# Paired score banks, B's values with 256 moving queries, and A's row sums applied after the values product

## The chip, the cores and the metric

The kernel runs on one core of a Trainium2 chip. The metric is the device time of one execution in microseconds (us), the median of several runs. All times here are us unless marked ns.

## What is computed

Two layers of an encoder over a sequence of S = 512 tokens with D = 1024 channels. Each layer has an attention part with two groups of heads and a gated feed-forward part (ConvGLU). What matters here is the attention part, shortened:

```python
h = rmsnorm(x, g_attn)
# h @ w_in gives q, k, v of group A and of group B; q, k get a per-head norm and rotary
# group A: 8 query heads, 2 key heads, dim 64, each block of 128 queries sees keys of 1 block to either side
scores = where(valid, q @ k.T * 64**-0.5, NEG)
m = maximum(max(scores), sink)
p = exp(scores - m)
p = p / (sum(p) + exp(sink - m))
out_a = p @ v
# group B: 4 heads, two score maps each (dim 64), values of dim 128, all 512 keys
p = softmax(q @ k.T * 64**-0.5)          # two maps: p0, p1
out_b = (p0 - lam * p1) @ v              # then a per-head norm, times a gain
x = x + concat(out_a, out_b) @ w_out
x = x + down(silu(conv(up_gate(norm(x)))) * up_value(norm(x)))
```

## The kernel before

**Arithmetic.** Every product is fp32 kept as a high and a low part (float32r), three matmuls for one (`mm3`, L193: high by high, high by low, low by high). `split_out` (L245) makes the two parts of a tile: ACT copies the source into the high part, DVE subtracts to get the low part. Where the source lies in PSUM, its bank is free only when both have read it. The residual is held transposed, eight tiles of 128 channels by 512 tokens. Weights come by DMA in units; ACT rounds a unit to its high part (L181) and DVE or POOL makes the low part (L182).

**Who sets the order.** Each engine runs its instructions in one fixed order. A scheduler sets it from the order in which the code emits them and from when their inputs and buffers come free in its own model of time. `weave` (L121) decides the order of emission: attention (`attend`, L580, with the weight `ATT` = 92) is mixed with a second track of weight 98.6, which is projection work for group B's two halves (`proj_b`, L614: values bv, queries bq, keys bk, four blocks of 128 tokens each) and then the output projection (`out_pass`, L627, passes 0 and 1; `out_tail`, L660). Each track yields numbers for the PE time of its pieces, and the one that is behind goes next. So matmuls of the second track (names pj_bv, pj_bq, pj_bk, wo) stand between attention's matmuls and fill the time in which attention waits.

**Group A** (L399 to L477) goes over two pairs of heads `ip` and four query blocks `qb`. `a_scores` writes four score tiles sc_a, each in a PSUM bank of its own (`at`), from 64-row matmuls: heads g = 0 and 1 lie in rows 0 to 63 and 64 to 127. DVE adds the mask and takes the maximum (L416), ACT takes the exponentials with their sums (so_a, L434), DVE adds the sink's exponential es_a and inverts the sums, and four DVE multiplications normalise the probabilities (L441). `a_values` transposes them on PE (pt_a, L457), splits them, multiplies by the values into pv_a, and splits pv_a by halves of 64 rows into yh and yl.

**Group B** (L488 to L577) goes over halves of two heads, query blocks and heads. `b_scores` writes two score tiles sc_b (L502), DVE takes two maxima (L505), ACT two exponentials (e_b, L509), DVE combines them (L517). `b_values` transposes the result (wt_b, L529), splits it and multiplies it with the values, the transposed probabilities stationary and 128 columns of values moving (L538 to L541). `b_norm` sums the squares on DVE, multiplies by the inverse root, transposes (tr_yb, L566) and splits.

**PSUM.** Eight banks of 128 x 512: `mm` two (projection and output projection), `at` four single ones (scores, A's and B's transposes), `acc` one (sums of a values product), `tq` one (transposes). The projection's queries and keys pass through `qk_out` (L324): ACT copies the product into raw (L331), which frees the mm bank, and squares it (L333); DVE sums; POOL takes the power -0.5 (L243); DVE multiplies keys by it (L342); POOL does the rotary (L348, L352, L353); PE transposes into the tq bank (tr_bq, tr_bk, L357), and `split_out` reads that bank.

**SBUF buffers** of interest: rp 7 tiles of 128 x 256, tmp 7 of 128 x 512, prob 6, yp 3.

## Time and profile before

| | |
|---|---|
| runs | 1309.32, 1310.32, 1308.12, median 1309.32 |
| profiled execution, its span from first to last instruction | 1302.4 |
| instructions in it | 17571 |
| PE busy in the span | 98% |
| DVE, ACT, POOL busy in the span | 59%, 43%, 30% |
| mean DMA rate | 79 GB/s |

The profile shows one execution. Its span is all of that execution's time that is shown; the median of the runs is 6.9 longer than it. A row of a timeline is: start, duration, engine, line of the kernel, operation, output <- inputs, shape. A row of a group adds the count and, after the bar, busy time and mean ns of one, and then idle time of the engine ahead of it and what ended it. xN marks records that lie on each other and were put into one. PE is TensorE (its matmuls are pipelined, and their ends are modelled, so starts are the better guide), PEld its weight loads, DVE the vector engine, ACT the scalar engine, POOL the GpSimd engine, SP the queue that issues DMAs.

### The profile page before, as it was taken

What the parts mean: (1) busy time and instruction counts of PE and PEld (TensorE: products, weight loads), DVE (VectorE), ACT (ScalarE), POOL (GpSimd) and SP (SyncE); (2) the same over time, 40 slices, a digit from 0 to 9 for tenths busy, and PEclk for the clock granted to TensorE, in tenths of its full rate; (3) what the DMA queues carried; (4) which work ended last, traced back from release to release, by engine and by line L of the source; (5) the groups of instructions that cost most, each with busy time, mean ns of one, the idle gap of its engine ahead of it and who ended that gap; (6) DMA issues with size and microseconds to landing.
All of it is one profiled execution on the core that took longest, in us unless ns stands there. A gap on an engine that the chain in (4) does not pass through costs nothing. (4 is left out here: it accounts for less than half of the span.)

```text
span 1302.4 us, 17571 instructions
## 1 busy us (share of the span) xinstructions
PE 1270.6 (98%) x6744; PEld 1056.6 (81%) x6744; DVE 772.9 (59%) x1425; ACT 557.5 (43%) x1027; POOL 385.4 (30%) x446
## 2 busy tenths in 40 slices
PE   6999899999999999999999999999899999999998
PEld 6988788687888888888899878877788888888887
DVE  7678787767655324554466786767765543355532
ACT  4566555435433223333455656544443332233321
POOL 6847376114211000110156654741411110011100
PEclk8999999999999999999999999999999999999999
DMA  5211112113332233332331211111133322433232
GB/s 181 91 33 49 58 33 65 33 33 97 98 97 85 85 106 97 98 97 79 100 98 66 65 33 33 56 59 33 33 113 97 97 81 94 117 98 98 79 106 90
DMA packets 32628, 102.96 MB, mean 79 GB/s; under 512 B 3616, under 2 KB 4000, under 8 KB 32544
## 3 DMA queue, kind: packets, MB, share of 16 engines
q1 hardware_dynamic: 32544, 101.84, 25.6%
q8 instruction: 53, 0.87, 0.3%
q14 instruction: 31, 0.25, 0.1%
HBM read 99.73 MB, written 2.10 MB: 78 GB/s over the span
## 5 line engine op out<-in xcount | busy, mean ns | idle before, releaser
L181 ACT CAST wh<-wr 128x1024 fp32r<-128x1024 f32 (+3 forms) x210 | 197.7, 944 | 400.1 <-PE up L195 192.0
L195 PE MATMUL up<-nf_l,wh 128*128 128x512 f32 x704 | 275.3, 391 | 2.3 <-DVE nf_l L213 1.9
L196 PE MATMUL up<-nf_h,wl 128*128 128x512 f32 x704 | 274.5, 390 | 1.2 <-DVE wl L182 0.9
L194 PE MATMUL up<-nf_h,wh 128*128 128x512 f32 x704 | 272.9, 390 | 0.0
L182 DVE TENSOR_TENSOR wl<-wr,wh 128x1024 fp32r<-128x1024 f32 (+3 forms) x174 | 193.3, 1114 | 112.2 <-ACT wh L181 111.8
L702 POOL TENSOR_TENSOR cv<-cv,rb 128x512 f32<-128x512 f32 x44 | 57.8, 1316 | 521.5 <-ACT cv L701 521.5
L195 PEld LDWEIGHTS up<-nf_l,wh 128*128 128x128 f32 x704 | 132.1, 188 | 33.6 <-DVE nf_l L213 6.6
L196 PEld LDWEIGHTS up<-nf_h,wl 128*128 128x128 f32 x704 | 132.1, 188 | 29.7 <-DVE wl L182 2.9
L194 PEld LDWEIGHTS up<-nf_h,wh 128*128 128x128 f32 x704 | 132.2, 188 | 27.6
L195 PE MATMUL dn<-act,wh 128*128 128x512 f32 x352 | 138.5, 394 | 0.0
L196 PE MATMUL dn<-act,wl 128*128 128x512 f32 x352 | 138.4, 394 | 0.0
L194 PE MATMUL dn<-act,wh 128*128 128x512 f32 x352 | 137.9, 393 | 0.0
L182 POOL TENSOR_TENSOR wl<-wr,wh 128x1024 fp32r<-128x1024 f32 x36 | 87.1, 2421 | 89.4 <-ACT wh L181 89.4
L695 DVE TENSOR_TENSOR gp<-up,rb 128x512 f32<-128x512 f32 x44 | 30.3, 693 | 103.4 <-PE up L196 101.8
L703 DVE TENSOR_TENSOR cv<-cv,up 128x512 f32<-128x512 f32 x44 | 30.2, 687 | 82.6 <-POOL cv L702 73.0
L194 PEld LDWEIGHTS dn<-act,wh 128*128 128x128 f32 x352 | 66.0, 188 | 16.0
L195 PEld LDWEIGHTS dn<-act,wh 128*128 128x128 f32 x352 | 66.0, 187 | 15.7
L196 PEld LDWEIGHTS dn<-act,wl 128*128 128x128 f32 x352 | 66.0, 188 | 15.4
L716 DVE TENSOR_TENSOR x<-x,dn 128x512 f32<-128x512 f32 x32 | 22.0, 689 | 78.4 <-PE dn L196 78.4
L509 ACT ACTIVATE e_b<-sc_b,mx_b,rqb 128x512 f32<-128x512 f32 x64 | 49.2, 774 | 38.6 <-DVE mx_b L506 38.6
L701 ACT ACTIVATE cv<-cv 128x512 f32<-128x512 f32 x44 | 27.8, 632 | 76.4 <-DVE cv L700 76.3
L505 DVE TENSOR_REDUCE mx_b<-sc_b 128x1 f32<-128x512 f32 x64 | 42.0, 681 | 0.2
(211 smaller groups left out, 2713.7 us busy)
## 6 DMA issues: line engine op xcount, KB each, us to landing
wr<-w_up SPq DMA_DIRECT2D x88, 512.0 KB, 3.6
wr<-w_in SPq DMA_DIRECT2D x36, 512.0 KB, 3.7
wr<-w_down SPq DMA_DIRECT2D x32, 384.0 KB, 3.1
wr<-w_down SPq DMA_DIRECT2D x32, 320.0 KB, 2.9
wr<-w_out SPq DMA_DIRECT2D x16, 512.0 KB, 3.6
x<-xT SPq DMA_DIRECT2D x8, 256.0 KB, 5.3
outT<-x SPq DMA_DIRECT2D x8, 256.0 KB, 2.0
rows<-row_par SPq DMA_DIRECT2D x2, 260.0 KB, 5.0
```

Source lines behind the costliest of these rows:

```text
L181: nc.scalar.copy(hi[:, o], raw[:, o])
L182: eng.tensor_tensor(out=lo[:, o], in0=raw[:, o], in1=hi[:, o], op=ALU.subtract)
L194: nc.tensor.matmul(acc, lhsT=a[0], rhs=b[0], start=start, stop=False)
L195: nc.tensor.matmul(acc, lhsT=a[0], rhs=b[1], start=False, stop=False)
L196: nc.tensor.matmul(acc, lhsT=a[1], rhs=b[0], start=False, stop=stop)
L505: nc.vector.tensor_reduce(out=mx[:, c:c + 1], in_=sc[c], axis=AX, op=ALU.max)
L509: nc.scalar.activation(e[c], sc[c], AF.Exp, bias=mx[:, c:c + 1], scale=rq[:, c:c + 1], accum_out=lsum[:, 2 * j + c:2 * j + c + 1])
L695: nc.vector.tensor_tensor(out=g[:, 1:S + 1], in0=acc[0], in1=rb, op=ALU.mult)
L701: nc.scalar.activation(cv, cv, AF.Silu)
L702: nc.gpsimd.tensor_tensor(out=cv, in0=cv, in1=rb, op=ALU.mult)
L703: nc.vector.tensor_tensor(out=cv, in0=cv, in1=acc[1], op=ALU.mult)
L716: nc.vector.tensor_tensor(out=x_sb[d], in0=x_sb[d], in1=acc, op=ALU.add)
```

## The change

- The four single `at` banks become two pairs (`at2`, a tile over two banks). The two 64-row score tiles of a step, in A and in B, lie in one pair, and one DVE reduction takes B's two maxima. The feed-forward part and the projections that used `at` take halves of a pair.
- Group A: the normalisation of the probabilities is gone. POOL copies the four inverse sums over 64 columns each (rx_a); after the values product PE turns rx_a by two plain fp32 matmuls with the identity (rt_a, in tq, L481 of the changed kernel), ACT copies that to SBUF (ry_a), DVE multiplies it with pv_a by halves (L487), and one split over 128 rows makes yh and yl. A's transposes pt_a go to a half of a pair for the first key block, to tq for the second, to mm for the third.
- Group B: the order of steps is now half, pair of query blocks, head, block in the pair. `b_weights` transposes and splits; `b_values` then multiplies once for two query blocks, values stationary and 256 moving columns. `b_norm` handles two query blocks and both heads at once: ACT scales and squares, PE sums the squares by four matmuls with a column of ones (ss_yb, L578), POOL takes the power, PE spreads the factors over rows by four matmuls (rt_yb, L586), DVE multiplies, and the split reads SBUF. The transposes tr_yb are gone.
- The output projection's gates wait on pairs of query blocks; tmp has 8 buffers, prob 4 of double size, the rotary tables share 3, yp is gone.

```diff
-        return sb.tile([P, S], F32R, tag="prob", bufs=6, name=name)
+        return sb.tile([P, 2, S], F32R, tag="prob", bufs=4, name=name)
...
-        return sb.tile([P, n], F32, tag="tmp", bufs=7, name=name)
+        return sb.tile([P, n], F32, tag="tmp", bufs=8, name=name)
...
-    def at(name):
-        return ps.tile([P, S], F32, tag="at", bufs=4, name=name)
+    def at2(name):
+        return ps.tile([P, 2, S], F32, tag="at", bufs=2, name=name)
...
+    def both(name):
+        t = at2(name)
+        return t[:, 0], t[:, 1]
...
-                sc = [at(f"sc_{nm}_{i}_{g}") for g in range(2)]
+                sc = both(f"sc_{nm}_{i}")
...
-            for i in range(4):
-                nc.vector.tensor_scalar(out=so[i][:, :n], in0=so[i][:, :n], scalar1=rl[:, i:i + 1], scalar2=None,
-                                        op0=ALU.mult)
-            a_so[ip, qb] = so
+            rx = rp(f"rx_{nm}")
+            nc.gpsimd.tensor_copy(rx.rearrange("p (i d) -> p i d", d=HD), rl.unsqueeze(2).broadcast_to([P, 4, HD]))
+            a_so[ip, qb] = so, rx
         def a_values(ip, qb):
             kb0, kb1 = max(qb - 1, 0), min(qb + 2, NT)
...
-            so = a_so.pop((ip, qb))
+            so, rx = a_so.pop((ip, qb))
...
-                tr = at(f"pt_{nm}_{b}")
+                tr = mm(f"pt_{nm}_{b}") if b == 2 else both(f"pt_{nm}_{b}")[0] if b == 0 else tq(f"pt_{nm}_{b}")
...
-                ph = prob(f"ph_{nm}_{b}")
-                pl = prob(f"pl_{nm}_{b}")
-                split_out(ph, pl, tr)
-                pb.append((ph, pl))
+                pt = prob(f"p_{nm}_{b}")
+                split_out(pt[:, 0], pt[:, 1], tr)
+                pb.append((pt[:, 0], pt[:, 1]))
...
+            rt = tq(f"rt_{nm}")
+            for i in range(2):
+                nc.tensor.matmul(rt[:, i * P:(i + 1) * P], lhsT=rx[:, i * P:(i + 1) * P], rhs=ident,
+                                 start=True, stop=True)
+            ry = tmp(f"ry_{nm}")
+            nc.scalar.copy(ry[:, :CW], rt[:, :CW])
             for g in range(2):
                 rs = slice(g * HD, (g + 1) * HD)
-                o = slice(qb * P, (qb + 1) * P)
-                split_out(ya[ip][0][rs, :, o], ya[ip][1][rs, :, o],
-                          pv[rs, g * 2 * P:(g + 1) * 2 * P].rearrange("p (a q) -> p a q", q=P))
+                nc.vector.tensor_tensor(out=ry[rs, CW:], in0=ry[rs, :CW], in1=pv[rs, g * CW:(g + 1) * CW], op=ALU.mult)
+            o = slice(qb * P, (qb + 1) * P)
+            split_out(ya[ip][0][:, :, o], ya[ip][1][:, :, o], ry[:, CW:].rearrange("p (a q) -> p a q", q=P))
+            yield 0.25
...
-            if j == 0:
-                b_st[half, qb] = small(f"bl{l}_{half}_{qb}", 4)
...
-            sc = [at(f"sc_{nm}_{c}") for c in range(2)]
+            sc2 = at2(f"sc_{nm}")
+            sc = (sc2[:, 0], sc2[:, 1])
             for i, (u, v) in enumerate(((0, 0), (0, 1), (1, 0))):
                 for c in range(2):
                     rs = slice(c * HD, (c + 1) * HD)
                     nc.tensor.matmul(sc[c], lhsT=q[u][rs, j, qb * P:(qb + 1) * P], rhs=k[v][rs, j, :],
                                      start=i == 0, stop=i == 2)
-            for c in range(2):
-                nc.vector.tensor_reduce(out=mx[:, c:c + 1], in_=sc[c], axis=AX, op=ALU.max)
+            nc.vector.tensor_reduce(out=mx, in_=sc2, axis=AX, op=ALU.max)
...
-        def b_values(half, qb, j):
+        def b_weights(half, qb, j):
             h = 2 * half + j
...
             w = b_st.pop((half, qb, j))
-            tr = (mm if half and j else at)(f"wt_{nm}")
+            if qb % 2 == 0:
+                b_st[half, j, "w"] = [prob(f"w{n}_b{l}_{h}_{qb}").rearrange("p a (b q) -> p (a b) q", b=2)
+                                      for n in "hl"]
+            wt = b_st[half, j, "w"]
+            tr = (mm(f"wt_b{l}_{h}_{qb}") if half and j else both(f"wt_b{l}_{h}_{qb}")[0])
             for b in range(NT):
                 nc.tensor.transpose(tr[:, b * P:(b + 1) * P], w[:, b * P:(b + 1) * P], ident)
-            wh, wl = prob(f"wth_{nm}"), prob(f"wtl_{nm}")
-            split_out(wh, wl, tr)
+            o = slice(qb % 2 * P, qb % 2 * P + P)
+            split_out(wt[0][:, :, o], wt[1][:, :, o], tr.rearrange("p (b q) -> p b q", b=NT))
             yield 0.5
...
+
+        def b_values(half, qp, j):
+            if j == 0:
+                b_st[half, qp, "acc"] = accum(f"yb{l}_{half}_{qp}")
+            yb = b_st[half, qp, "acc"][:, j * CW:(j + 1) * CW]
+            wt = b_st.pop((half, j, "w"))
+            for b in range(NT):
+                vh, vl = (v[:, b % 2 * CW + j * P:b % 2 * CW + j * P + P] for v in vb[half, b // 2])
+                mm3(yb, (vh, vl), (wt[0][:, b], wt[1][:, b]), b == 0, b == NT - 1)
+                if b % 2:
+                    yield 0.7
+
+        def b_norm(half, qp):
+            nm = f"yb{l}_{half}_{qp}"
+            yb = b_st.pop((half, qp, "acc"))
+            y = tmp(f"y_{nm}")
+            nc.scalar.activation(y, yb, AF.Copy, scale=cols[:, l, c3:c3 + 1])
+            sq = tmp(f"sq_{nm}")
+            nc.scalar.activation(sq, yb, AF.Square)
+            le = small(f"le_{nm}", 4)
+            lsum = b_st.pop((half, qp)).rearrange("p (i c) -> p i c", c=2)[:, :, 0]
             nc.vector.scalar_tensor_tensor(out=le, in0=lsum, scalar=EPS / (1.0 - lam_init) ** 2, in1=lsum,
                                            op0=ALU.mult, op1=ALU.mult)
...
+            yield 0.2
+            ss = tq(f"ss_{nm}")
+            for i in range(4):
+                nc.tensor.matmul(ss[:, i:i + 1], lhsT=sq[:, i * P:(i + 1) * P], rhs=ones, start=True, stop=True)
+            rr = small(f"rr_{nm}", 4)
+            nc.vector.scalar_tensor_tensor(out=rr, in0=ss[:, :4], scalar=1.0 / (P * (1.0 - lam_init) ** 2), in1=le,
+                                           op0=ALU.mult, op1=ALU.add)
+            rsqrt(rr, rr)
+            yield 0.5
+            rt = tq(f"rt_{nm}")
+            for i in range(4):
+                nc.tensor.matmul(rt[:, i * P:(i + 1) * P], lhsT=rr[:, i:i + 1].broadcast_to([P, P]), rhs=ident,
+                                 start=True, stop=True)
+            nc.vector.tensor_tensor(out=y, in0=y, in1=rt, op=ALU.mult)
+            if qp == 0:
...
+            yh, yl = (v[:, :, qp * CW:(qp + 1) * CW] for v in b_st[half, "y"])
+            split_out(yh, yl, y.rearrange("p (j q) -> p j q", j=2))
+            b_st["yb", half, qp] = True
+            yield 0.5
         def attend():
             seq = [("a", qb, ip) for ip in range(2) for qb in range(NT)]
-            seq += [(half, qb, j) for half in range(2) for qb in range(NT) for j in range(2)]
+            seq += [(half, 2 * qp + i, j) for half in range(2) for qp in range(2) for j in range(2) for i in range(2)]
...
-                    yield from b_values(kind, qb, j)
-                    while norms:
-                        yield from norms.pop(0)
-                    if j == 1:
-                        norms.append(b_norm(kind, qb))
-                        yield next(norms[0])
+                    return
+                yield from b_weights(kind, qb, j)
+                if norms:
+                    yield from norms.pop(0)
+                if qb % 2:
+                    yield from b_values(kind, qb // 2, j)
+                    if j:
+                        g = b_norm(kind, qb // 2)
+                        yield next(g)
+                        norms.append(g)
...
-            yield lambda: ("ya" if p == 0 else ("yb", 0, NT - 1)) in b_st
+            yield lambda: ("ya" if p == 0 else ("yb", 0, 1)) in b_st
...
-            yield lambda: ("yb", 1, 2 * half + 1) in b_st
+            yield lambda: ("yb", 1, half) in b_st
...
-            yield lambda: ("yb", 1, 1) in b_st
+            yield lambda: ("yb", 1, 0) in b_st
```

What this does to the order. PE's order in the first layer, where group A's steps (sc_a, pv_a, pt_a, rt_a) stand among group B's projection (pj_bk, and the transposes tr_bq of its queries). Before:

```order
L412 MATMUL sc_a_1_1_0_1_1508<-ka_213,qal_1_418 128x384
L195 MATMUL pj_bk_1_1519<-wl_1101,na_h_139 128x256
L357 MATMUL tr_bq_2_1320<-ident,raw_bq_2_1308 128x128 x2
L196 MATMUL pj_bk_1_1519<-wh_1100,na_l_140 128x256
L194 MATMUL pj_bk_1_1519<-wh_1100,na_h_143 128x256
L194 MATMUL pv_a_0_3_1421<-ph_a_0_3_0_1427,va_214 128x512
L195 MATMUL pj_bk_1_1519<-wl_1101,na_h_143 128x256
L196 MATMUL pj_bk_1_1519<-wh_1100,na_l_144 128x256
L194 MATMUL pj_bk_1_1519<-wh_1100,na_h_147 128x256
L195 MATMUL pj_bk_1_1519<-wl_1101,na_h_147 128x256
```

And after, at the transposes of the same block of queries:

```order
L208 MATMUL pj_bk_1_1483<-wh_1084,na_l_148 128x256
L369 MATMUL tr_bq_2_1302<-ident,raw_bq_2_1290 128x128 x2
L481 MATMUL rt_a_0_2_1326<-ident,rx_a_0_2_1056 128x128 x2
L369 MATMUL tr_bq_3_1371<-ident,raw_bq_3_1359 128x128 x2
L469 MATMUL pt_a_0_3_0_1430<-ident,so_a_0_3_0_0_1176 128x128
L469 MATMUL pt_a_0_3_0_1430<-ident,so_a_0_3_1_0_1187 128x128
L469 MATMUL pt_a_0_3_0_1430<-ident,so_a_0_3_0_1_1178 128x128
L469 MATMUL pt_a_0_3_0_1430<-ident,so_a_0_3_1_1_1189 128x128
L469 MATMUL pt_a_0_3_1_1438<-ident,so_a_0_3_0_0_1176 128x128
```

Before, projection matmuls stand on both sides of tr_bq_2; after, tr_bq_2, A's rt_a, tr_bq_3 and pt_a follow each other, and tr_bq_2, rt_a, tr_bq_3 and the second pt_a share the one tq bank.

ACT's order at the copy raw_bk_0, which frees the mm bank of the first block of B's keys, with A's exponentials (so_a) and copies. Before:

```order
L246 CAST yh_0_779<-pv_a_0_2_1252 64x2x128
L331 ACTIVATE raw_bk_0_1480<-pj_bk_0_1443,na_r 128x256
L333 ACTIVATE sq_bk_0_1482<-raw_bk_0_1480 128x256
L246 CAST ph_a_0_3_0_1427<-pt_a_0_3_0_1422 128x512
L431 ACTIVATE es_a_1_0_1407<-dn_a_1_0_1405 128x4
L434 ACTIVATE so_a_1_0_0_0_1357,ls_a_1_0_1409<-so_a_1_0_0_0_1357,ng_a_1_0_1402,rqa_413 128x256
L434 ACTIVATE so_a_1_0_0_1_1359,ls_a_1_0_1409<-so_a_1_0_0_1_1359,ng_a_1_0_1402,rqa_413 128x256
```

After:

```order
L258 CAST bqh_0_792<-tr_bq_2_1302 128x2x128
L484 COPY ry_a_0_2_1329<-rt_a_0_2_1326 128x256
L258 CAST bqh_0_792<-tr_bq_3_1371 128x2x128
L258 CAST yh_0_775<-ry_a_0_2_1329 128x2x128
L258 CAST p_a_0_3_0_1435<-pt_a_0_3_0_1430 128x512
L258 CAST p_a_0_3_1_1443<-pt_a_0_3_1_1438 128x512
L444 ACTIVATE es_a_1_0_1417<-dn_a_1_0_1415 128x4
L447 ACTIVATE so_a_1_0_0_0_1343,ls_a_1_0_1419<-so_a_1_0_0_0_1343,ng_a_1_0_1412,rqa_411 128x256
L447 ACTIVATE so_a_1_0_0_1_1345,ls_a_1_0_1419<-so_a_1_0_0_1_1345,ng_a_1_0_1412,rqa_411 128x256
L447 ACTIVATE so_a_1_0_1_0_1383,ls_a_1_0_1419<-so_a_1_0_1_0_1383,ng_a_1_0_1412,rqa_411 128x256
L447 ACTIVATE so_a_1_0_1_1_1385,ls_a_1_0_1419<-so_a_1_0_1_1_1385,ng_a_1_0_1412,rqa_411 128x256
L343 ACTIVATE raw_bk_0_1458<-pj_bk_0_1399,na_r 128x256
```

The copy raw_bk_0 stood ahead of A's exponentials and now stands behind them and behind six copies.

PE's order at the start of group B's second half (scores sc_b_2 and sc_b_3, weights' transposes wt_b, output projection wo). Before:

```order
L529 MATMUL wt_b_0_3_2809<-ident,e_b_0_3_0_2588 128x128 x4
L502 MATMUL sc_b_3_0_0_2856<-bkh_1_1785,bqh_1_1783 128x512
L566 MATMUL tr_yb_0_1_2694<-ident,y_yb_0_1_2565 128x128 x2
L502 MATMUL sc_b_2_0_0_2782<-bkl_1_1786,bqh_1_1783 128x512
L502 MATMUL sc_b_2_0_1_2783<-bkl_1_1786,bqh_1_1783 128x512
L502 MATMUL sc_b_2_0_0_2782<-bkh_1_1785,bql_1_1784 128x512
L502 MATMUL sc_b_2_0_1_2783<-bkh_1_1785,bql_1_1784 128x512
L502 MATMUL sc_b_3_0_0_2856<-bkl_1_1786,bqh_1_1783 128x512
L502 MATMUL sc_b_3_0_0_2856<-bkh_1_1785,bql_1_1784 128x512
L194 MATMUL wo_0_5_2988<-yh_0_779,wh_2379 128x512
```

After:

```order
L522 MATMUL sc_b_3_0_2779<-bkh_1_1747,bqh_1_1745 128x512 x2
L522 MATMUL sc_b_3_0_2779<-bkl_1_1748,bqh_1_1745 128x512 x2
L522 MATMUL sc_b_3_0_2779<-bkh_1_1747,bql_1_1746 128x512 x2
L548 MATMUL wt_b_2_0_2807<-ident,e_b_2_0_0_2682 128x128 x4
L578 MATMUL ss_yb_0_1_2820<-ones,sq_yb_0_1_2774 128x1 x4
L522 MATMUL sc_b_3_1_2837<-bkh_1_1747,bqh_1_1745 128x512 x2
L522 MATMUL sc_b_3_1_2837<-bkl_1_1748,bqh_1_1745 128x512 x2
L522 MATMUL sc_b_3_1_2837<-bkh_1_1747,bql_1_1746 128x512 x2
L548 MATMUL wt_b_2_1_2869<-ident,e_b_2_1_0_2718 128x128 x4
L548 MATMUL wt_b_3_0_2931<-ident,e_b_3_0_0_2788 128x128 x4
L206 MATMUL wo_0_6_2945<-yh_0_775,wh_2640 128x512
L207 MATMUL wo_0_6_2945<-yl_0_776,wh_2640 128x512
```

Before, the scores' matmuls of two heads were mixed, with output-projection matmuls (wo_0_5) behind the first of them; after, the two row halves of one score follow each other as one row with x2, and the output projection (wo_0_6) stands behind all four scores.

More of the change, by code (lines that the diff above doesn't have):

```diff
@@ L34 @@
 RP = 7
-YP = 3
 SMP = 12
@@ L376, in akv_done @@
             qk_out(raw[:, :P], t, P, tabs[1], ka, "ka", None)
-        run(project("akv", akv_done, at))
+        run(project("akv", akv_done, halves(both)))
         rqa = sb.tile([P, NT, 4, 2], F32, tag="rqa", bufs=1, name=f"rqa{l}")
@@ L387 @@
         qk = {}
-        banks = iter((mm, mm, at, at, at, at, mm, mm))
+        pairs_at = halves(both)
+        banks = iter((mm, mm, pairs_at, pairs_at, pairs_at, pairs_at, mm, mm))
         run(proj_a(0, lambda name: next(banks)(name)))
@@ L666 @@
               (chain(proj_b(0), proj_b(1), out_pass(0, mm), out_pass(1, mm), out_tail()), 98.6))
-        run(out_last(1, w_last, wide))
+        run(out_last(1, w_last, halves(wide2)))
         norm.square(NK - 2)
@@ L707 @@
             last = pi == len(FF_PARTS) - 1
+            wide = halves(wide2)
             for d in range(NK):
```

79 lines of the change are left out of this document (22 added, 57 removed).

## The prediction

> **What bounds the kernel now.** I read the page's busy shares first, then the table by stretches of 100 us, then the timeline inside the attention stretches, then the tile views of what passes through the few PSUM banks there. The shares:
>
> ```profile
> PE 1270.6 (98%) x6744; PEld 1056.6 (81%) x6744; DVE 772.9 (59%) x1425; ACT 557.5 (43%) x1027; POOL 385.4 (30%) x446
> ```
>
> PE is busy 98% of the span, so the end is set by what PE has to issue plus the time in which it waits. The stretches that the change touches, columns PE, PEld, DVE, ACT, POOL, granted clock, DMA share, GB/s:
>
> ```profile
> 100.00:200.00 100.00, 95.80 (x652) 80.19 (x652) 79.76 (x194) 58.70 (x147) 64.18 (x67) 1.00 0.15 46
> 200.00:300.00 100.00, 95.81 (x532) 75.52 (x532) 73.44 (x150) 49.22 (x100) 34.46 (x28) 0.98 0.16 48
> 700.00:800.00 100.00, 97.78 (x663) 83.36 (x662) 73.83 (x216) 60.32 (x154) 49.72 (x47) 0.98 0.17 51
> 800.00:900.00 100.00, 98.25 (x585) 78.90 (x583) 70.90 (x163) 53.01 (x118) 50.18 (x45) 0.98 0.14 43
> 900.00:1000.00 100.00, 96.50 (x490) 79.92 (x489) 68.30 (x102) 44.46 (x68) 24.97 (x31) 0.98 0.25 75
> ```
>
> Even here PE is busy: its idle time is 4.20 + 4.19 + 2.22 + 1.75 + 3.50 = 15.9 us. So work taken from DVE, ACT or POOL gains nothing by itself, work taken from PE counts in full, and a new wait of PE costs in full unless other work stands in PE's order at that place. DVE is at 70 to 80% in these stretches, so a chain through DVE, ACT and POOL is long, and only PE's filler hides it.
>
> **What PE loses and gains.** Ends of matmuls are modelled, so I price by the distance between starts. The values product before, moving 128, and a product with 256:
>
> ```profile
> 240.85 0.28 PE L539 MATMUL yb<-vb,wth_b 128*128 128x128 f32 x1
> ...
> 241.52 0.28 PE L539 MATMUL yb<-vb,wth_b 128*128 128x128 f32 x1
> ...
> 281.25 0.40 PE L649 MATMUL wo<-yl_b,wh 128*128 128x256 f32 x2
> 281.49 0.40 PE L649 MATMUL wo<-yh_b,wh 128*128 128x256 f32 x2
> ```
>
> Six steps take 0.67, so 0.111 each; two of 256 take 0.24, so 0.120 each. B's values go from 384 matmuls of 128 to 192 of 256: 42.6 to 23.0, **-19.6**.
>
> Score matmuls, first alone between wide products, then of both row halves together:
>
> ```profile
> 243.02 0.40 PE L194 MATMUL wo<-yh,wh 128*128 128x512 f32 x1
> 243.34 0.49 PE L502 MATMUL sc_b<-bkh,bqh 64*128 64x512 f32 x1
> 243.68 0.39 PE L502 MATMUL sc_b<-bkl,bqh 64*128 64x512 f32 x1
> 243.91 0.39 PE L502 MATMUL sc_b<-bkh,bql 64*128 64x512 f32 x1
> 244.24 0.50 PE L195 MATMUL wo<-yl,wh 128*128 128x512 f32 x1
> ...
> 154.82 0.72 PE L502 MATMUL sc_b<-bkh,bqh 64*128 64x512 f32 x2
> 155.16 0.62 PE L502 MATMUL sc_b<-bkl,bqh 64*128 64x512 f32 x2
> 155.39 0.61 PE L502 MATMUL sc_b<-bkh,bql 64*128 64x512 f32 x2
> ```
>
> A slot is 0.23 (243.68 to 243.91), and two matmuls of different row halves share one (155.16 to 155.39 with x2). Going from 128 rows to 64 and back lengthens three steps, to 0.32, 0.34 and 0.33, so by 0.09 + 0.11 + 0.10 = about 0.29 an episode. In the order, before has 58 such pairs and 268 single ones in 114 episodes, after has 190 pairs and 4 single ones in 58. B's slots go from 167 to 97: 70 x 0.23 = -16.2. A's go from 159 to 97; at 256 or 384 moving columns I take 0.148, between 0.120 and 0.175 (midway between 0.12 and 0.23): 62 x 0.148 = -9.2. Episodes: 56 x 0.29 = -16.1. Together **-41.5**.
>
> Added: 32 matmuls that turn A's reciprocals (L481), 32 that sum B's squares (L578) and 32 that spread B's factors (L586), in plain fp32. The nearest row:
>
> ```profile
> 317.79 1.05 PE L673 MATMUL rps<-ident,nf_r 128*128 128x128 f32 x8
> ```
>
> Four matmuls of the code are eight passes there; the record covers seven steps and a last duration of 0.27, so (1.05 - 0.27) / 7 = 0.111 a pass. 96 matmuls are 192 passes, +21.3; B's 32 transposes go, -3.6. Sum **+17.7**; were the sums of squares, which move one column, to cost nothing, it would be 10.6, and I keep the upper end because the short matmuls above pay 0.111 whether they move 128 or twice that. PE's issue changes by -19.6 - 41.5 + 17.7 = **-43.4**, with ends at -50.5 and, were the halves not to run together, -43.4 + 25.4 = -18.
>
> **What comes off DVE.** The four normalisations of A's probabilities (L441) and some small sums go:
>
> ```profile
> L441 DVE TENSOR_SCALAR so_a<-so_a,rl_a 128x256 f32<-128x256 f32 (+1 forms) x64 | 36.9, 636 | 0.0
> ```
>
> 36.9 us off a DVE that isn't the bound: nothing by itself. It shortens the step from A's reciprocals to its transposes, which is counted in the chains below.
>
> **The waits that come in.** Before, four single banks, two mm banks and one tq bank serve attention and projections. After, the four are two pairs; A's transposes of the second key block, A's reciprocal matmuls and the q/k transposes of the projection all pass through the one tq bank; and in the order after they stand next to each other on PE with no projection matmul between (the rows in the section on the change). Each must wait until the one before it has been read twice:
>
> ```profile
> L246 ACT CAST bqh<-tr_bq x16: 352/372/374, 95.8 to 827.3; 128x256 fp32r<-128x256 f32 x16
> L247 DVE TENSOR_TENSOR bql<-tr_bq,bqh x16: 406/414/425, 96.8 to 827.7; 128x256 fp32r<-128x256 f32 x16
> ```
>
> Transposes 0.11 + 0.27, copy 0.37, subtraction 0.41, with the hand-overs 1.25 us at the least. The second chain is on ACT: raw_bk_0, which frees the mm bank that the next projection needs, now stands behind six copies, the sink's exponential and four exponentials of A. What the chain is made of:
>
> ```profile
> L416 DVE CUSTOM_DVE_ANT_0 so_a<-sc_a,mask_sb 128x256 f32<-128x256 f32 x15 | 6.0, 409 | 0.4 <-PE pt_a L457 0.4
> L247 DVE TENSOR_TENSOR pl_a<-pt_a,ph_a 128x512 fp32r<-128x512 f32 x18 | 12.1, 682 | 1.0 <-ACT ph_a L246 1.0
> 747.62 0.59 ACT L434 ACTIVATE so_a<-so_a,ng_a,rqa 128x256 f32<-128x256 f32 x1
> ...
> 748.21 0.59 ACT L434 ACTIVATE so_a<-so_a,ng_a,rqa 128x256 f32<-128x256 f32 x1
> ...
> L331 ACT ACTIVATE raw_bk<-pj_bk,na_r 128x256 f32<-128x256 f32 x4 | 1.9, 476 | 0.0
> L243 POOL TENSOR_TENSOR rs_bk<-sv_bk,nhalf 128x4 f32<-128x4 f32 x4 | 4.1, 1016 | 7.1 <-DVE sv_bk L339 7.1
> L342 DVE TENSOR_TENSOR raw_bk<-raw_bk,rs_bk 128x256 f32<-128x256 f32 x4 | 4.4, 1104 | 1.9 <-POOL rs_bk L243 1.9
> L352 POOL TENSOR_TENSOR raw_bk<-raw_bk,tab 128x256 f32<-128x256 f32 x4 | 3.0, 739 | 0.2
> L182 POOL TENSOR_TENSOR wl<-wr,wh 128x1024 fp32r<-128x1024 f32 x8 | 19.1, 2389 | 13.5 <-ACT wh L181 13.5
> 95.38 0.38 PE L357 MATMUL tr_bq<-ident,raw_bq 128*128 128x128 f32 x2
> ...
> 135.10 0.38 PE L357 MATMUL tr_bk<-ident,raw_bk 128*128 128x128 f32 x2
> ```
>
> I walk the order after from tr_bq_2 to tr_bk_0, in us from tr_bq_2. tq free 1.25; A's reciprocals through it, with their ACT copy, 2.4; tr_bq_3 then takes tq, and DVE, which holds three masked maxima (0.41 each) and two half multiplications (0.36 each, an estimate under the 0.41 above) ahead of bql, frees it at 3.65. A's two transposes are split by DVE (0.68 each) at 5.1 and 6.1; the sink's exponential follows at 6.5; four exponentials at 0.585 end at 8.8; raw_bk_0 ends at 9.3; two power operations on POOL (1.0 each), POOL's new copy of the reciprocals (0.7, an estimate by the nearest POOL row of that size), one DVE multiplication and six rope operations (0.7 each) end at 16.25, and tr_bk_0 can go. PE's own work in between is 10.6 by the prices above: it waits **5.7**. From tr_bq_0 to tr_bq_2 the same walk, with two weight halves of 2.39 on POOL ahead of the rope, gives 20.5 against 13.8: **6.7**. From tr_bk_0 to tr_bk_2, with 384-wide exponentials, 16.7 against 7.8: **8.9**. Sum 21.3 a layer, 42.6 for both. Before, the stretch from tr_bq_0 to tr_bk_2 took 135.10 - 95.38 = 39.7; by this walk it takes 53.5.
>
> The second place is the start of B's second half, from tr_bk_3 on: four score pairs through two pairs of banks, with out-projection work behind them instead of between:
>
> ```profile
> 240.58 1.28 DVE L505 TENSOR_REDUCE mx_b<-sc_b 128x1 f32<-128x512 f32 x2
> L509 ACT ACTIVATE e_b<-sc_b,mx_b,rqb 128x512 f32<-128x512 f32 x64 | 49.2, 774 | 38.6 <-DVE mx_b L506 38.6
> L517 DVE SCALAR_TENSOR_TENSOR e_b<-e_b,al_b,e_b 128x512 f32<-128x512 f32 x32 | 29.4, 918 | 0.1
> ```
>
> A round is maximum 1.28 (two reductions in one record; one instruction after, the same elements), two exponentials 1.55, hand-overs 0.5 and part of DVE's next weights, about 4 us: 16.1 for four against 8.7 of PE work, **7.4** a layer, 14.8. Other direct turnarounds (A's first transposes, the factors of B's norm before tr_bk_3) I put at 6 to 7 a layer, an estimate with the 1.25 as its unit: 13. Of the idle time of before nothing should stay as it is, since B's last norm is now covered by the last passes of the output projection:
>
> ```profile
> 284.28 0.41 PE L566 MATMUL tr_yb<-ident,y_yb 128*128 128x128 f32 x2 [1.13 <-DVE y_yb L562]
> ```
>
> That takes off 16. **The sum**: -43.4 + 42.6 + 14.8 + 13 - 16 = +11. Made against the profiled span of 1302.4 it gives 1313; the median of the runs, 1309.3, lies 6.9 above that span, and I carry this over: 1320. The new waits W break even at 43.4 + 16 = 59.4; I count 70.4.
>
> **The rivals.**
> *Only direct turnarounds (faster).* The walk assumes that DVE and ACT take their instructions with no slack. If the queue ahead of raw_bk_0 is done while PE still has work, what stays is the bare turnaround, which the order asks for at 30 places in tq: 1.25 less 0.45 of PE work between, 24 in all, and by the same count 10 in the pairs and 2 in mm: 36. -43.4 + 36 - 16 = -23, or **1286**. For it: DVE loses 50 us, and 98% of PE's time was covered before. Against: the order, which has no filler at those places.
> *The evacuation queue (slower).* A transposition of before, whose bank nobody waits for, is read late:
>
> ```profile
> 96.84 0.41 DVE L247 TENSOR_TENSOR bql<-tr_bq,bqh 128x256 fp32r<-128x256 f32 x1
> ...
> L357 PE MATMUL tr_bk<-ident,raw_bk x32: 270/272/328, 124.1 to 858.6; 128*128 128x128 f32 x32
> L247 DVE TENSOR_TENSOR bkl<-tr_bk,bkh x16: 406/414/426, 128.6 to 859.3; 128x256 fp32r<-128x256 f32 x16
> ```
>
> The first tr_bq takes 1.87 from its start at 95.38 to the end of bql, the first tr_bk 4.9 (124.1 to 128.6 and 0.41). If DVE stays so far behind, the turnarounds of tq are not 1.25 but between these two; with 1.0 more on each of 30 places that is +30 on 1320, **1350**. It decides where DVE is over some 80% busy around these transposes; the 79.76 of 100 to 200 us is near.
> [...]
> *The pairs don't run together.* The change puts halves next to each other; if they are issued one by one, 70 x 0.23 + 62 x 0.148 = 25.4 comes back: **1346**. The 58 pairs of before speak against it.
>
> **How the numbers follow.** A difference of 0.2%, 2.6 us, is about what a measurement of this kernel can tell from none. My forecast, waits between 55 and 85: 0.45, of which 0.37 is slower, 0.06 the same, 0.02 faster. Only direct turnarounds: 0.32, spread from 1280 to 1306. Evacuation queue: 0.18. No pairs: 0.05. So faster 0.34, same 0.06, slower 0.60. The likeliest alone reaches from 1305 to 1335; since faster and slower both hold much, the range takes in the case of direct turnarounds and half of the queue's: 1281 to 1350.
>
> **What would show it.** In the profile after: PE's instructions fall by some 130, its idle time in 100 to 300 and 700 to 1000 us rises from 16 to about 70, with waits of PE on bql, ry, pj_bk and tr_bk named in the waits; tr_bq_0 to tr_bk_2 takes over 50 us; sc_b shows as x2 throughout at 0.23. I am wrong on the waits if that stretch stays below 42 us or PE's idle time there is below 50; wrong on PE's work if yb steps at 256 are not near 0.12, or the fp32 matmuls take other than two passes.

## The result and the profile after

The changed kernel takes **1384.4 us** (1382.3 to 1386.2, four runs) against 1309.8 of the kernel before in the same session: 1.0572 times as long, interval 1.0557 to 1.0586. The forecast was 1320, slower, with a range to 1350: the sign was right, the size was not. The profiled execution's span is 1380.5, 78.1 longer than the 1302.4 of before.

PE's row on the page after:

```profile
PE 1276.0 (92%) x6712; PEld 1056.7 (77%) x6712; DVE 729.5 (53%) x1297; ACT 553.0 (40%) x1003; POOL 390.1 (28%) x454
```

PE has 32 records fewer and yet is busy 5 us longer, and it is idle for 104.5 us where it was for 31.8. The table by stretches, here cut at the stages of each kernel: for each layer, from A's first score to the last matmul of B's keys, and from there to the first matmul of the feed-forward part. Before:

```profile
55.30:201.00 145.70, 141.14 (x965) 119.44 (x965) 113.71 (x297) 86.61 (x217) 89.28 (x93) 0.99 0.15 46
201.00:292.60 91.60, 88.94 (x504) 71.06 (x503) 65.04 (x142) 40.94 (x87) 27.60 (x22) 0.98 0.16 47
696.60:839.10 142.50, 140.28 (x965) 119.74 (x965) 107.93 (x295) 86.96 (x214) 79.38 (x77) 0.99 0.15 45
839.10:930.90 91.80, 88.30 (x504) 71.67 (x502) 61.10 (x138) 40.20 (x86) 27.24 (x21) 0.96 0.16 46
```

After:

```profile
61.00:218.80 157.80, 132.92 (x915) 113.21 (x914) 80.23 (x233) 79.30 (x196) 83.60 (x90) 0.92 0.13 42
218.80:321.90 103.10, 90.07 (x532) 72.80 (x532) 75.28 (x142) 48.19 (x98) 34.23 (x26) 0.93 0.14 42
737.80:896.80 159.00, 136.77 (x914) 115.87 (x914) 78.96 (x232) 79.45 (x196) 80.52 (x84) 0.89 0.13 40
896.80:1003.40 106.60, 92.64 (x534) 73.62 (x533) 77.24 (x143) 48.53 (x99) 33.35 (x24) 0.90 0.13 40
```

Two columns changed. PE's idle time (length less busy) went from 4.6 + 2.7 + 2.2 + 3.5 = 13.0 to 24.9 + 13.0 + 22.2 + 14.0 = 74.1. And the granted clock, 0.96 to 0.99 before, is 0.89 to 0.93. Taking (1 - clock) times length as the time that PE lost to its clock, that is 8.4 before and 12.6 + 7.2 + 17.5 + 10.7 = 48.0 after. The four stretches are 526.5 - 471.6 = 54.9 longer: +61.1 idle, +39.6 clock, and what is left, -45.8, is PE's work (an estimate, since some idle time also lies at the lower clock). The other 23 us lie outside attention: 16.1 in the two feed-forward parts (378.2 + 373.4 against 367.7 + 367.8) and 6.8 in the first projections (54.6 + 37.7 against 49.1 + 36.4).

The waits of PE that answer to the prediction's walk, columns total, times, longest:

```profile
PE tr_bq L369 <- POOL raw_bq L365: 9.5, 4, 3.5
PE tr_bk L369 <- POOL raw_bk L365: 8.2, 4, 3.6
PE rt_a L481 <- DVE bql L259: 3.7, 4, 0.9
PE rt_a L481 <- DVE bkl L259: 3.7, 4, 0.9
```

and the same places on PE's timeline:

```profile
105.00 0.44 PE L369 MATMUL tr_bq<-ident,raw_bq 128*128 128x128 f32 x2 [1.55 <-POOL raw_bq L365]
106.36 0.71 PE L481 MATMUL rt_a<-ident,rx_a 128*128 128x128 f32 x4 [0.92 <-DVE bql L259]
107.62 0.41 PE L369 MATMUL tr_bq<-ident,raw_bq 128*128 128x128 f32 x2 [0.55 <-ACT ry_a L484]
128.18 0.44 PE L369 MATMUL tr_bq<-ident,raw_bq 128*128 128x128 f32 x2 [3.52 <-POOL raw_bq L365]
145.71 0.44 PE L369 MATMUL tr_bk<-ident,raw_bk 128*128 128x128 f32 x2 [1.27 <-POOL raw_bk L365]
162.89 0.69 PE L369 MATMUL tr_bk<-ident,raw_bk 128*128 128x128 f32 x2 [2.12 <-POOL raw_bk L365]
```

tr_bq, rt_a, tr_bq follow each other at 1.36 and 1.26: the turnaround of the one tq bank, in which projection and attention go in lockstep. Where PE's clock is down it is longer, 1.78 at the next such place (129.54 to 131.32; the clock was 0.50 from 130 to 135). From tr_bq_0 (105.00) to tr_bk_2 (162.89) it is 57.9, in steps of 23.2, 17.5 and 17.2 where the walk had 20.5, 16.3 and 16.7. This stretch as a whole, and the same one in the second layer:

```profile
105.00:162.89 57.89, 42.88 (x254) 34.54 (x254) 24.99 (x77) 25.05 (x62) 29.78 (x33) 0.85 0.12 37
782.87:842.10 59.23, 45.58 (x253) 36.21 (x254) 24.54 (x77) 25.21 (x62) 29.80 (x33) 0.80 0.13 36
```

PE is idle for 15.0 and 13.7 of them, and (1 - clock) times length is 8.7 and 11.8. And what such a place does to the clock, in stretches of 5 us around the first of them:

```profile
95.00:100.00 5.00, 5.00 (x38) 4.37 (x37) 1.49 (x7) 3.75 (x11) 0.40 (x1) 1.00 0.00 0
100.00:105.00 5.00, 3.45 (x31) 3.21 (x29) 0.84 (x4) 0.89 (x2) 4.84 (x7) 1.00 0.00 0
105.00:110.00 5.00, 3.16 (x17) 2.40 (x17) 3.61 (x14) 1.96 (x5) 1.35 (x2) 0.82 0.01 3
110.00:115.00 5.00, 5.00 (x20) 3.19 (x19) 2.40 (x8) 3.98 (x12) 0.40 (x1) 0.50 0.00 0
115.00:120.00 5.00, 5.00 (x41) 4.87 (x39) 1.74 (x2) 2.64 (x4) 2.04 (x2) 1.00 0.00 0
```

From 110 to 115 PE is busy throughout and waits for nothing, but its clock is at half: 20 matmuls where 38 and 41 run in the rows around it. Most of the clock's bill for the waits at 103 to 109 comes after they are over: by (1 - clock) times length, 0.9 from 105 to 110 and 2.5 from 110 to 115.

### The profile page after: what moved, and what is told of

It is laid out like the page before. It is cut to its first block, busy times and chain, and to the rows that moved or that the text cites. A ratio compares the mean times of both kernels' runs of the same rounds, so it can differ in the third digit from the quotient of the medians.

```text
span 1380.5 us, 17377 instructions
## 1 busy us (share of the span) xinstructions
PE 1276.0 (92%) x6712; PEld 1056.7 (77%) x6712; DVE 729.5 (53%) x1297; ACT 553.0 (40%) x1003; POOL 390.1 (28%) x454
## 4 chain that ended last, share of the span: by engine, by line
PE 64%; DVE 6%; ACT 4%; POOL 2%; issue 1%; POOLq 0%; ACTq 0%; DVEq 0%
PE up L208 8%; PE up L207 8%; PE up L206 7%; PE dn L207 4%; PE dn L206 4%; PE dn L208 4%; ACT so_a L447 1%; ACT wh L193 1%; DVE mx_b L524 1%; PE wo L206 1%; PE wo L207 1%; DVE wl L194 1%; ACT e_b L528 1%; PE sc_b L522 1%; PE wo L208 1%
## 5 line engine op out<-in xcount | busy, mean ns | idle before, releaser
L207 PE MATMUL up<-nf_l,wh 128*128 128x512 f32 x464 | 181.2, 391 | 3.4 <-DVE nf_l L225 3.3
L208 PE MATMUL up<-nf_h,wl 128*128 128x512 f32 x464 | 180.7, 390 | 0.0
L206 PE MATMUL up<-nf_h,wh 128*128 128x512 f32 x464 | 180.7, 389 | 0.0
L207 PEld LDWEIGHTS up<-nf_l,wh 128*128 128x128 f32 x464 | 87.1, 188 | 23.5 <-DVE nf_l L225 5.7
L206 PE MATMUL dn<-act,wh 128*128 128x512 f32 x240 | 95.6, 398 | 6.4 <-ACT wh L193 3.5
L208 PEld LDWEIGHTS up<-nf_h,wl 128*128 128x128 f32 x464 | 87.1, 188 | 18.2 <-DVE wl L194 0.4
L206 PEld LDWEIGHTS up<-nf_h,wh 128*128 128x128 f32 x464 | 87.1, 188 | 18.0
L207 PE MATMUL dn<-act,wh 128*128 128x512 f32 x240 | 95.4, 398 | 0.4 <-DVE act L259 0.4
L208 PE MATMUL dn<-act,wl 128*128 128x512 f32 x240 | 94.6, 397 | 0.0
L206 PEld LDWEIGHTS dn<-act,wh 128*128 128x128 f32 x240 | 45.0, 188 | 20.7 <-ACT wh L193 5.6
L207 PEld LDWEIGHTS dn<-act,wh 128*128 128x128 f32 x240 | 45.5, 190 | 11.8 <-DVE act L259 1.1
L206 PE MATMUL pj_bv<-wh,na_h 128*128 128x256 f32 x128 | 38.5, 301 | 5.5 <-ACT raw_bk L343 3.6
```

Source lines behind the costliest of these rows:

```text
L206: nc.tensor.matmul(acc, lhsT=a[0], rhs=b[0], start=start, stop=False)
L207: nc.tensor.matmul(acc, lhsT=a[0], rhs=b[1], start=False, stop=False)
L208: nc.tensor.matmul(acc, lhsT=a[1], rhs=b[0], start=False, stop=stop)
```

## The experiments

**The parts alone.** Each of the first three starts from the kernel before and takes over one part; the fourth starts from the kernel after.

e1, the paired score banks alone (A's and B's transposes in a single bank of the pairs' ring, the first projections and the feed-forward part in mm and the same ring):

```diff
-                sc = [at(f"sc_{nm}_{i}_{g}") for g in range(2)]
+                sc = both(f"sc_{nm}_{i}")
...
-            sc = [at(f"sc_{nm}_{c}") for c in range(2)]
+            sc = both(f"sc_{nm}")
```

> The kernel before with nothing but the paired score banks: the two 64-row halves of a score in one tile over two banks, everything else in single banks, A's normalisation, B's values and B's norm as before. Theory T (the one bank tq is what hurts: A's reciprocals and transposes pass through it between the projection's transposes, the two tracks go in step, PE waits and then runs at a lower clock): tq is used as before here, so the waits stay near the 32 us of before and PE's shared slots count: 1275 to 1300, granted clock in 100 to 200 us at 0.95 or more. Rival P (two double banks in place of four single ones set the waits): 1330 or more, with PE's idle time in the attention stretches at 50 us or more.

1353.3, ratio 1.0371 (1.0345 to 1.0397): theory T fell here, the pairs lose by themselves, as rival P had it: PE is idle for 64.1 in the attention stretches (13.0 in the kernel before). The largest of PE's waits:

```profile
PE pt_a L464 <- DVE so_a L448: 21.2, 17, 3.4
```

A's transposes wait for the normalised probabilities; in the kernel before this wait came to 1.5. The clock is 0.965 over the span (0.991 before).

e2, A's row sums alone (the L441 multiplications replaced by rx, rt in tq, ry and the multiplication of pv, as in the change):

> The kernel before with nothing but A's inverse row sums moved behind the values product (reciprocals through POOL, two matmuls into tq, an ACT copy and DVE multiplications); the four single banks, A's transposes in them, and B as before. Theory T: the order again puts the projection's transposes and the reciprocals next to each other in tq, so this part alone costs about half of the loss in the attention stretches: 1325 to 1350, with the stretch from the first score of A to the last matmul of B's keys 10 to 17 us longer in each layer and the clock there at 0.93 or less. Rival P: no change beyond the 7 us of added matmuls, 1305 to 1318.

1363.8, ratio 1.0454 (1.0427 to 1.0481), more than T expected, and not where T had it. The stretch to B's last key is 8.7 and 8.2 longer (T: 10 to 17) at a clock of 0.94 and 0.95 (T: 0.93 or less), the one behind it 19 and 23: the loss is not confined to the place where tq is shared. That attention comes out of that place late, so that its remainder runs with less of the other track beside it, is argued and not shown.

e3, B's values and norm alone:

> The kernel before with nothing but B's part: values product with 256 moving queries, the norm for two query blocks by matmuls, the new order of steps; single banks, A as before. By PE's work it is 19.6 less for the values and 10.6 more for the norm, so 1300. Theory T: 1290 to 1312, since tq is used by B's norm only after the projection is nearly done. Rival V (B's longer norm and its order make the waits in the second half of the attention): 1325 or more, all of it between the last matmul of B's keys and the first of the feed-forward part.

1307.0, ratio 1.0017 (0.9993 to 1.0040): no difference. The losses of e1 and e2 (+46 and +57) with e3's 0 come to more than the +75 of all three, so the parts don't add.

e4, the kernel after, with `wide` taking one bank at a time (mm, or a tile of one bank in the pairs' ring) for the feed-forward part, the last output pass and the first projections:

```diff
-                acc = wide2(f"up{l}_{f}")
...
+                    a = wide(f"up{l}_{f}_{j}")
...
-            wide = halves(wide2)
```

> The changed kernel, but the first projections, the last output pass and the feed-forward part take single banks instead of halves of a pair. Theory H (in a pair, the second half is not written before the first has been read, so the order brings the first two matmuls of a later tile forward, and their weights come late): the feed-forward stretches lose their 16 us and the first projections some 5: 1360 to 1368. Rival (the waits of the feed-forward part come from a weight stream that is late after the attention): 1380 to 1388.

1364.4. Each set against the kernel before in its own session, this is 17 less than the kernel after (1.0445 against 1.0572). Feed-forward went from 751.6 to 741.6, the first projections from 92.3 to 88.5. In the kernel after, PE's first matmul into the second half of the last dn pair waits for DVE, which reads the first half (the first two rows below). In earlier pairs two matmuls of the next pair stand ahead of it in the order, and their weights are not there yet (the third row): waits of dn for wh come to 6.2 in nine places.

```profile
692.23 0.69 DVE L737 TENSOR_TENSOR x<-x,dn 128x512 f32<-128x512 f32 x1 [2.12 <-PE dn L208]
693.06 0.47 PE L206 MATMUL dn<-act,wh 128*128 128x512 f32 x1 [0.87 <-DVE x L737]
471.07 0.50 PE L206 MATMUL dn_2a<-act,wh 128*128 128x512 f32 x1 [0.74 <-ACT wh L193]
```

With single tiles the order has dn_0 to dn_7 one after the other again, and no dn matmul waits (in e4's first feed-forward part they start 0.23 apart from 461.89 to 474.55). Theory H holds for 14 us; feed-forward and first projections stay 9 above the kernel before, and no run takes that apart.

**What a wait does to the clock.** m1 and m2 are kernels of their own, one execution each:

```python
for r in range(reps):
    v = sb.tile([P, S], F32R, tag="s", bufs=4, name=f"s{i}")
    nc.scalar.activation(v, a, AF.Copy, scale=0.5)
    for q in range(k):
        ...
        nc.vector.tensor_scalar(out=u, in0=v, scalar1=0.99, scalar2=None, op0=ALU.mult)
    a = burst(n, f"b{n}_{k}_{r}", s)
```

> A kernel of its own that leaves the whole computation out: trains of 8, 16 or 32 matmuls of 128 x 512 (1.8, 3.7, 7.4 us), each waiting for an ACT copy and 0, 2, 4 or 7 DVE passes on the train before, some 45 us of each pattern, 60 matmuls in one piece ahead of each. It shows what PE's waits do to its granted clock. Theory C (the clock falls to half with the share of time that PE is idle, not only after one long gap): patterns with gaps of 1 to 3 us show 0.5 to 0.9 wherever PE is busy less than some two thirds of the time, and the steps in them go from 0.23 to 0.43. Rival (only a single long gap counts): the clock stays at 1.0 for all gaps under 3 us, and the lower clock in the changed kernel has another cause.

Trains of 8 matmuls with gaps of 0.75, 1.75, 2.75 and 4.13 us, then trains of 32 with 1.70 and 4.13 (the later two thirds of each pattern):

```profile
34.90:62.70 27.80, 21.04 (x81) 14.57 (x82) 0.00 (x0) 5.37 (x9) 0.00 (x0) 1.00 0.00 0
91.80:116.90 25.10, 14.59 (x57) 10.29 (x58) 5.12 (x12) 3.58 (x6) 0.00 (x0) 1.00 0.00 0
145.50:180.40 34.90, 20.91 (x49) 14.49 (x50) 8.54 (x20) 2.99 (x5) 0.00 (x0) 0.65 0.00 0
214.60:242.00 27.40, 15.01 (x33) 10.45 (x34) 8.96 (x21) 1.79 (x3) 0.00 (x0) 0.56 0.00 0
...
571.50:606.80 35.30, 30.14 (x129) 24.06 (x130) 2.56 (x6) 1.79 (x3) 0.00 (x0) 1.00 0.00 1
692.40:729.40 37.00, 28.73 (x96) 22.25 (x96) 5.98 (x14) 1.19 (x2) 0.00 (x0) 0.80 0.00 0
```

Gaps to 1.75 kept the full clock in these stretches even where PE was busy for 58% of the time, which theory C had at 0.5 to 0.9; with trains of 8, a gap of 2.75 brought it to 0.65, which the rival had at 1.0. So neither held as it was put. Trains of 32 had 1.00 with gaps of 1.70 and 0.80 with 4.13. At its start the pattern of 8 with 1.75 did lose the clock: its second train (82.57) took 3.75 and the third (88.03) 2.08, with no change in the pattern. It stayed open why the kernel after, whose gaps in the lockstep at 105 us are 0.4 to 1.6, lost its clock.

> The trains of the first clock kernel with short ones, the whole computation left out again: 1 to 16 matmuls of 128 x 512 (0.23 to 3.7 us) against gaps of 0.75 (no DVE pass) to 3.3 us (5 passes). In the first one, trains of 1.7 us kept the full clock with gaps of 1.75 (PE at work half of the time) and lost it with gaps of 2.75. Theory C1 (the share of idle time counts, as in the lockstep of the changed kernel, whose gaps were under 2 us): trains of 1 and 2 matmuls with gaps of 0.75 to 1.2 us, PE at work for 25 to 40 %, run at a clock of 0.7 or less. Theory C2 (one gap must be longer than some 2 us): they run at 1.0, and only the rows with 3 or 5 passes fall.

Trains of 1, 2 and 4 matmuls with a gap of 0.75, of 8 with 1.15, of 4 and of 6 with 1.75:

```profile
36.30:69.70 33.40, 18.26 (x24) 7.01 (x25) 0.00 (x0) 13.13 (x22) 0.00 (x0) 0.50 0.00 0
101.90:140.50 38.60, 24.38 (x41) 10.49 (x42) 0.00 (x0) 11.34 (x19) 0.00 (x0) 0.50 0.00 1
171.40:215.80 44.40, 33.20 (x65) 19.11 (x66) 0.00 (x0) 8.96 (x15) 0.00 (x0) 0.50 0.00 0
...
432.10:460.30 28.20, 19.01 (x73) 13.20 (x74) 3.42 (x8) 4.78 (x8) 0.00 (x0) 1.00 0.00 0
488.90:525.10 36.20, 20.44 (x41) 12.16 (x42) 7.69 (x18) 5.37 (x9) 0.00 (x0) 0.50 0.00 0
555.30:580.50 25.20, 12.95 (x49) 8.63 (x50) 5.98 (x14) 4.18 (x7) 0.00 (x0) 1.00 0.00 0
```

C1's forecast came true for short trains: up to 4 matmuls (0.9 us at full clock) between gaps of 0.75 ran at half clock (0.50) once it had fallen, which took up to 12 us; 4 with 1.75 did so too (0.50), while 6 (in m2) or 8 (in m1) had 1.00 at gaps of 1.75. Its reason, the share of idle time, did not. Before their clock fell, trains of 4 with 0.75 had PE busy for 62% of the time (7.18 of 11.65 us from 157.20); trains of 6 with 1.75 had it busy for 51% (12.95 of 25.20) and kept it. The length of the trains counts beside the gaps (at 1.75, 0.50 with 4 matmuls and 1.00 with 6); what exactly the clock goes by stays open. The lockstep, two to eight short matmuls between waits, looks like the case of short trains, but it is also a passage from dense work to gaps, at which the trains of 8 with 1.75 lost the clock for a while. Which of the two it is was not shown.

**Which bank.** From here on all kernels with pairs have e4's single tiles. e6 takes A out of tq, with both of its first transposes in one pair (`pt2[b]`) and the reciprocals in mm; e12 and e13 do the two apart:

```diff
-            rt = tq(f"rt_{nm}")
+            rt = mm(f"rt_{nm}")
```

> The changed kernel with single tiles in the first projections and the feed-forward part, and with A out of tq: A's transposes in both halves of one pair, its reciprocals in an mm bank; tq serves the projection and B's norm alone. Beside it stands the same kernel with A in tq, 1364. Theory T (the shared tq bank is the main wait): 1300 to 1325. Theory Q (the pairs alone make attention's own chain too long for the work that fills it, and the longer of the two chains decides): 1335 to 1360, since the pairs alone gave 1353.

> The kernel of 1364 (the changed kernel with single tiles in the first projections and the feed-forward part), with one line changed: A's reciprocals through an mm bank; A's second transposes stay in tq. In its order projection matmuls stand between the projection's transposes again. If the reciprocals are what puts the two tracks in step (they come last in A's step, behind the values product, so tq is held for the whole of it): 1315 to 1335. If the transposes do it: 1355 or more.

> The kernel of 1364 with A's second transposes in the other half of the pair that holds its first, and the reciprocals left in tq. Its order still has the projection's transposes, the reciprocals and the next transposes in a row. If the reciprocals put the tracks in step: 1345 or more; if the transposes do: 1325 or less.

| kernel | reciprocals | second transposes | time |
|---|---|---|---|
| e4 | tq | tq | 1364.4 |
| e13 | tq | pair | 1352.7 |
| e12 | mm | tq | 1328.7 |
| e6 | mm | pair | 1323.1 |

e6 lies in T's range, near its upper end. The reciprocals' bank is the larger part: that one line takes 35.6 off, the transposes 11.6; both runs came out in the range given for the reciprocals. PE's timeline of e12 at the first four transposes of B's queries:

```profile
105.95 0.44 PE L369 MATMUL tr_bq<-ident,raw_bq 128*128 128x128 f32 x2
110.43 0.44 PE L369 MATMUL tr_bq<-ident,raw_bq 128*128 128x128 f32 x2
120.76 0.44 PE L369 MATMUL tr_bq<-ident,raw_bq 128*128 128x128 f32 x2
124.20 0.44 PE L369 MATMUL tr_bq<-ident,raw_bq 128*128 128x128 f32 x2
```

No wait stands before any of them, and the third comes 14.8 after the first instead of 23.2.

**Without a part, and the weave.** e7 leaves out the row sums (pairs and B's values stay). e8, e9 and e10 are e3, e6 and e7 with attention's total in the weave (`ATT`) at 84, 86 and 84, near the sum of what its pieces now yield; e11 has no pairs, B's values, and the row sums with the reciprocals in mm.

> The changed kernel without the move of A's row sums (probabilities normalised as before, transposes in slots of the pairs), with single tiles in the first projections and the feed-forward part: the paired scores and B's values together. Theory T: tq isn't shared, 1270 to 1300. Theory Q: the pairs' loss stays, less what B's values save: 1335 to 1355, with most of PE's waits on the normalised probabilities, as in the run with the pairs alone.

> B's values alone (as in the third run, where 1307 against 1307 gave no difference), with attention's total in the weave set to 84, near the sum that its pieces now yield, in place of 92: output-projection work then stands between the scores of B's second half. If that part's gain of 9 us in PE's work was lost to waits for want of filler: 1290 to 1300. If it wasn't: 1305 to 1310 again.

> The kernel of 1323 (A out of tq, single tiles, all three parts of the change) with attention's total in the weave at 86, the sum that its pieces yield. As with B's values alone, where this took 6 us: 1312 to 1320. If what is left is the pairs' own waits: 1320 to 1327.

> The kernel of 1326 (paired scores and B's values, A as before, single tiles) with attention's total at 84. By the same rule 1315 to 1322; if what is left is the pairs' own waits, 1323 to 1330.

> No pairs: the four single banks of before, with B's values and A's row sums on the output, the reciprocals through an mm bank, attention's total at 86. PE's work is that of the 1301 kernel and 7 more; DVE has 37 less to do. Theory (a shared tq bank made the row sums cost 57, not the row sums): 1295 to 1312. Rival (the longer way of A's output costs wherever its bank is): 1325 or more.

| kernel | pairs | row sums | B's values | ATT | time | ratio, interval |
|---|---|---|---|---|---|---|
| e7 | yes | no | yes | 92 | 1326.0 | 1.0172 (1.0131 to 1.0213) |
| e8 | no | no | yes | 84 | 1301.3 | 0.9960 (0.9941 to 0.9979) |
| e9 | yes | in mm | yes | 86 | 1311.3 | 1.0036 (1.0021 to 1.0051) |
| e10 | yes | no | yes | 84 | 1316.0 | 1.0066 (1.0041 to 1.0091) |
| e11 | no | in mm | yes | 86 | 1309.1 | 1.0015 (1.0002 to 1.0028) |

The kernel before took 1305.5 to 1309.8 in the different sessions, so differences between runs of two sessions are good to some 4 us. The weave's number is worth 6 to 12 (7 to 14 by the ratios): the change left it at 92 although its pieces yield less. That attention was therefore issued too far ahead of the work that should fill its waits is argued. e7 came out between its two ranges, 1326 where T ended at 1300 and Q began at 1335; e8 fell just between its ranges too. Row sums cost 8 (e11 less e8) with the reciprocals in mm, about the 7.1 of their matmuls, and not the 57 of e2. e2 also differs from e11 in the weave's number and in B's part; the bank by itself is the 35.6 of e12. Pairs still cost 14.6 (e10 less e8), 9.8 of it in the attention stretches. The span's rows say how: PE is idle for 64.5 in e10 and 39.1 in e8 (+25), and (1 - clock) times the span is 38 at 0.971 against 23 at 0.982 (+15), so PE's work is some 25 less and the waits and the clock take more. e8, B's values alone with the weave adjusted, beats both kernels by a little: 0.4% under the one before. No run has the kernel before with another number in the weave, so how much of this is the values is not shown.

## Why the prediction was right and wrong

- **PE's work, -43.4.** Right, as far as the account goes: the attention stretches leave -45.8 once idle time and clock are taken off. B's values step at 0.12 (nine steps from 242.12 to 243.20). Eight fp32 passes take 0.82 (291.11 to 291.93), 0.10 a pass, and the sums of squares, which move one column, pay that too. The instructions fell by 32 and not by 130: each of the 96 added matmuls is two records, and the sign had counted one. The pairs run together (sc_b as x2 at 180.36 and 180.59 in the trace after, 0.23 apart), so the rival in which they don't is out.

```profile
180.36 0.40 PE L522 MATMUL sc_b<-bkl,bqh 64*128 64x512 f32 x2
180.59 0.40 PE L522 MATMUL sc_b<-bkh,bql 64*128 64x512 f32 x2
```

- **The new waits, 70.4.** Right in sum, but by luck: two errors in it cancel. PE is idle 74.1 in the attention stretches (67.2 in the 500 us that the prediction named). In the place of the walk the waits are 15.0 + 13.7 = 28.7, not 42.6; all other idle time there is 45.4, where the sum had 14.8 + 13. The length of that stretch, 57.9 and 59.2 for the walk's 53.5, came near because PE did part of its work there at half clock. That the old idle time goes (-16) is inside these numbers.
- **The step that failed** stands at the head of the working: "a new wait of PE costs in full", which the sum took as its own length and no more, with every price at full clock. PE came out of the waits at half clock and ran its next work at that (0.50 from 110 to 115 and from 130 to 135): some 40 us in the attention stretches that the sum did not have. About half of them lie in the two stretches of the walk, where they took the place of waiting that the walk had counted. m2 shows short trains between short gaps at half clock (1 to 4 matmuls with gaps of 0.75: 0.50); that it is just 40 us is accounted from the clock column, not shown by a run that keeps the waits and the clock.
- **A part that was not priced.** The pairs outside attention (the first projections and the feed-forward part) got no term. These places took 23 more; e4's single tiles took 14 of it back there.
- 11 + 40 + 23 = 74 against the 78 of the two spans. The other 4 is what waits and work came out at, 61.1 - 45.8 = +15 for the sum's +11.
- **The rival "only direct turnarounds"**, with the most of the chance for faster, is out: the walk's queues on ACT, DVE and POOL were there, with waits of up to 3.6 for POOL's raw_bq and raw_bk. "The evacuation queue" named the right side and too small a size. It put 1.0 on each turnaround of 1.25; they measured 1.26 to 1.37 at full clock and up to 1.78 where PE itself was slow (rt_a's row took 1.09 to 1.23 there and 0.71 at full clock), and PE's idle time within them is the same 0.92 and 0.55 everywhere, so DVE's queue is not what made up the difference (DVE is busy for 48.1 us between 100 and 200, where it was for 79.8).
- **The paired scores:** the slots are shared (the rows at 180.36 and 180.59), and net of that the pairs still lose 14.6 (e10 less e8).
- What stays open is why two pairs lose to four single banks. e1 and e10 show that they do and where PE waits (21.2 for so_a in e1, 10.7 for p_a in e10); that a score pair holds half of the ring until DVE or ACT has read both halves is only argued. In e1 and e10 a transposition of A or B takes a place in the same ring of two as well, so how much of the loss is the scores' and how much the transposes' is open too.

## What to carry to other kernels

Price a new wait of PE at its length and then ask what the clock does behind it: by the clock column, the new waits here came with about two thirds as much again (39.6 beside 61.1 of new idle time). A bank that is handed out in the code's order ties together whatever passes through it, so before sending one more short tile through a single bank, move it to another in a trial: that one line was worth 36 us. When a ring of buffers changes shape, follow all its users, also those far from the change, and refit the weave's totals to what the pieces now yield.

## What the runs showed of the hardware

In m2 PE's clock was 0.50 with gaps of 0.75 us when the trains between them had 1, 2 or 4 matmuls of 128 x 512, and in the later part of each pattern it was 1.00 with gaps of 1.75 when they had 6 (m2) or 8 (m1). In the kernel after it came back within some 6 us of the last wait before dense work (pt_a at 108.96; 0.50 from 110 to 115, 1.00 from 115 to 125). A plain fp32 matmul that moves one column took as long as one that moves 128, two passes of 0.10 (ss_yb at 291.11, rt_yb at 296.71, each eight passes in 0.82).
